# A decoder layer on one core: operands of seven-product units given back one by one, a pair-wise attention state, and other blocks for the left operands' sums

## The chip, the cores and the metric

The kernel runs on 1 core of one Trainium2 chip. The metric is the device time of one execution in microseconds (us), as the median of several runs. Five engines work at once: TensorE (PE in the profile; PEld is its weight load), VectorE (DVE), ScalarE (ACT), GpSimd (POOL) and SyncE (SP), which issues the transfers. Each engine takes its own instructions strictly in its listed order.

## What is computed

One layer of a decoder, 1024 positions of 1024 channels in float32. All matrices are float32 in HBM.

```python
h = rmsnorm(x, pre_mix_g);  z = h @ w_in          # 7696 columns
# z: GLA q,k (256 each), v, out-gate (512 each), forget (16); short conv B,C,x (512 each);
#    dilated q,k,v (1536 each)
y_gla = gla_branch(...)       # linear attention: state = state*decay + k^T v, o = q state + intra part
y_sc  = sc_b * causal_dwconv(sc_c * sc_x)
y_dil = dilated_branch(...)   # rotary q,k; three strided windows
gates = sigmoid(h @ w_gate + b_gate)              # 3 x 1024 columns
x = x + rmsnorm(sum(gates * (branch @ w_branch)) @ w_mix_out)
h = rmsnorm(x, pre_ffn_g)
y = (gelu(causal_dwconv(h @ w_ff_gate) + b) * (h @ w_ff_up)) @ w_ff_down   # 2816 wide
x = x + rmsnorm(y, post_ffn_g)
```

## The kernel before, in words

A float32 product is made of three matmuls: each operand is split into a rounded part (`wh`, a ScalarE copy, L158) and the rest (`wl`, a VectorE subtraction, L159), and high x high, high x low and low x high are added up in PSUM.

**Units of seven products.** Large projections go in units of 256 columns (`seven`, L266 to L323). A unit cuts its 1024 x 256 weights and the activations into 2 x 2 blocks and makes the result from seven block products in place of eight. The activations' block sums (`T`, `FT`) are made once per stage; the weights' sums s1 (L279), s2 (L281), s1' (L283) and A11 - A21 (L285) are made by GpSimd for each unit. The seven operands (A11, A12, s1, s2, s1', A11 - A21, A22, numbered 0 to 6) are each split by L158 and L159. A product is 12 matmuls of 512 columns (L295). On TensorE a unit's products run in the order

    X0 of this unit, X6 of the unit before, Y1, Z2, X3, Z4, X5

where X, Y and Z are PSUM banks and the digit is the operand. X accumulates on: X6 adds to what X5 left, so it can't start until VectorE has read X after X5 (the addition into c22, L315). Between X5 and X6 TensorE has only X0 of the next unit. Z4 is read by the addition into c12 (L313), Y1 by the one into c11 (L304). Each finished quarter goes to a `use` function.

**Places of the operands.** Before, operands 0 to 3 of a unit lie in one pair of tiles (`wh`, `wl`) and 4 to 6 in another, two tiles of each kind in all:

```python
for i in range(2):
    sets.append([wp.tile([128, 4, 4, 128], F32R, name=n, tag=n) for n in ("wh", "wl")])
op = lambda i: (sets[i // 4][0][:, i % 4], sets[i // 4][1][:, i % 4])
```

A tile is written again only when every reader of it is done: operands 0 to 3 of the next unit wait for X3, and 4 to 6 of a unit for X6 of the unit before, which runs behind X0. The raw weights (`raw`, three buffers of 512 KB, loaded by SyncE) come free when the last split of their unit is done.

**Where units run.** Thirty in the input stage (about 75 to 660 us): short conv and gates (the `use` of the short conv's x is L455 and on), then the block that makes cosine and sine on VectorE and ScalarE (L466 to L484), then 12 "turned" units (dilated q and k) mixed with 7 light gate units, then two for the GLA q and k. A turned unit's `use` (`rope_out`, L494) makes, for each quarter, two ScalarE copies of half the partitions (L498, L499), a product with cosine on VectorE (L505), a product with sine on GpSimd (L506) and a VectorE addition (L507). Twenty units run in the feed-forward network (FFN, about 1370 to 1765 us): for c = 1 to 10 one of the gate, whose `use` makes the convolution (L1278 to L1283), and one of the up projection, whose `use` multiplies and calls `forms`.

**`forms` (L1289)** makes left operands for the down projection: a store of quarter a11, of a22 and of a12 as each is made, and at the last quarter four GpSimd results (L1295), each stored: number 5 into a22 (which the store `keep(c, 4, a22)` still reads), 7 into a21, 6 into a11, 3 into a12.

**GLA scan (L797 to L826).** For each of 8 blocks of 128 positions and each of 4 heads: an intra product (L805, 128 rows of weights, 128 columns) and, from block 1, a product with the state (L807, 64 rows, 128 columns), alternating; then four products of 64 weight columns for the new state (L812), and two VectorE operations for it (L817). A float32 matmul call is two passes in the profile. After the scan: `rstd` on VectorE, then per piece a VectorE scaling (L836), a GpSimd product (L838) and four transposes on TensorE (L842).

**What sets the order.** The program states the work in the order of the code; a scheduler at build time then sets the order on each engine, by priorities and by when places come free. So a change of places moves instructions on all engines.

Of the kernel before, what the change touches and what calls it, by code (L numbers as in the profile page):

```python
# [72 lines left out]
def trunk(ctx: ExitStack, tc, x, positions, w_in, w_alpha_up, b_alpha, gla_norm_g, sc_conv_w,  # L73
# [12 lines left out]
    def pt(tag, name):  # L86
        return psum.tile([128, 512], F32, name=name, tag=tag,
                         bufs={"g": 4, "s": 2, "t": 1, "o": 1}[tag])

    def slot(tag, shape, dt=F32, name=None):  # L90
        return main.tile(shape, dt, name=name or tag, tag=tag)
# [174 lines left out]
    def seven(src, c0, B, Ts, tmp, dst, use):  # L266
# [5 lines left out]
        s1, s2 = [t.rearrange("p (k c) -> p k c", k=4) for t in tmp]  # L272
        sets = []
        for i in range(2):
            sets.append([wp.tile([128, 4, 4, 128], F32R, name=n, tag=n) for n in ("wh", "wl")])
        op = lambda i: (sets[i // 4][0][:, i % 4], sets[i // 4][1][:, i % 4])
        split(*op(0), A11)
# [41 lines left out]
        def rest():  # L319
            prod(X, op(6), tt(3), False)  # L320
            use(1, 0, X)
        pending.append(rest)


# [107 lines left out]
    block_sums(H, fr, TS)  # L432
    gemm_by_part(first_units, H, "gt", 256, lambda c, h, ps: gate_out(0)(c, h, ps, ring()))


# [354 lines left out]
    for bp in range(4):  # L790
# [5 lines left out]
        ins = S.activation(kin[:, 2 * bp:2 * bp + 2], p.rearrange("p (b c) -> p b c", c=256), AF.Copy)  # L796
    ssg = sm.tile([128, 32], F32, name="ssg", bufs=1)  # L797
    state = None
    states = slot("t2", [128, 2, 2, 128], name="states")
    for b in range(8):  # L800
        po = [pt(tag, "go")[:, :256].rearrange("p (a e) -> p a e", a=2) for tag in "ot"]
        for h in range(4):
            bs = slice((h % 2) * 64, (h % 2) * 64 + 64)
            p = po[h % 2][:, h // 2]
            PE.matmul(p, Sb[:, b, h], gv[:, b, h * 128:h * 128 + 128], start=True, stop=b == 0)  # L805
            if b:
                PE.matmul(p, qk[bs, h // 2, b * 128:b * 128 + 128], state[bs, h // 2], start=False, stop=True)  # L807
        if b < 7:
            p2 = pt("s", "gst")[:, :256].rearrange("p (a e) -> p a e", a=2)
            for h in range(4):  # L810
                bs = slice((h % 2) * 64, (h % 2) * 64 + 64)
                PE.matmul(p2[bs, h // 2], kin[:, b, h * 64:h * 64 + 64], gv[:, b, h * 128:h * 128 + 128],  # L812
                          start=True, stop=True)
            new = states[:, b % 2]
            for a in range(2):
                if b:
                    V.scalar_tensor_tensor(new[:, a], state[:, a], dec[:, a, b:b + 1], p2[:, a],  # L817
                                           op0=OP.mult, op1=OP.add)
                else:
                    V.tensor_copy(new[:, a], p2[:, a])  # L820
            state = new
        for h in range(4):
            S.activation(gv[:, b, h * 128:h * 128 + 128], po[h % 2][:, h // 2], AF.Square,
                         accum_out=ssg[:, 4 * b + h:4 * b + h + 1])
        for w in range(2):
            V.tensor_copy(gv[:, b].rearrange("p (a w e) -> p a w e", w=2, e=128)[:, :, w], po[w])  # L826
    rg = rstd(ssg, 128, 32)
# [461 lines left out]
    def forms(c, y, il):  # L1289
# [12 lines left out]
        if il == (1, 0):  # L1302
            keep(c, 2, a12)
            made(5, a22, a21, a22, OP.add)
            made(7, a21, a11, a21)
            made(6, a11, a22, a11)
            made(3, a12, a12, a11)

# [16 lines left out]
    for il in ((0, 0), (1, 1), (1, 0)):  # L1325
        forms(0, ys, il)

    ring = halves_ring(("t2", "t0", "t1"))
    yring = Ring([fb[:, i] for i in (0, 1, 3)])
# [194 lines left out]
```

## Time and profile before

| what | value |
|---|---|
| median of 3 runs (their range) | 1985.59 us (1982.05 to 1987.25) |
| the profiled execution | 1988.03 us, span 1986.2 us |
| TensorE busy / weight loads | 1900.2 us (96%) / 1602.9 us (81%) |
| VectorE / ScalarE / GpSimd busy | 66% / 44% / 38% |
| mean granted clock of TensorE | 0.986 |

Busy time counts an instruction from its start to its modelled end; a busy TensorE can still be at a lower clock. "Idle before, releaser" is the time in which the engine did nothing ahead of an instruction, and the instruction that let it go on. Idle time of an engine other than TensorE costs something only where TensorE waits behind it.

### The profile page before, as it was taken

The page shows a single profiled execution, that of the slowest core. Times are in us where ns is not written, and L with a number is a line of the kernel's source. Part 1 is how long each engine was busy: PE and PEld are TensorE (multiplying, and loading weights), DVE is VectorE, ACT ScalarE, POOL GpSimd, SP SyncE. Part 2 cuts the span into 40 slices and gives each one's busy share as a digit, 9 for nine tenths or more (in the row PEclk, how much of TensorE's full clock was granted, in tenths as well). Part 3 has the DMA queues.
Part 4 walks back from the last instruction along what each step waited for, and adds up shares of the span by engine and source line. Part 5 has one row for each costly group of instructions (what it writes and reads, how often), then busy time and mean ns, then how long its engine had stood idle before and what let it go on. Part 6 is the DMA issues. An engine that isn't in the chain of part 4 may idle for free.

```text
span 1986.2 us, 26265 instructions
## 1 busy us (share of the span) xinstructions
PE 1900.2 (96%) x9705; PEld 1602.9 (81%) x9705; DVE 1312.6 (66%) x1913; ACT 875.6 (44%) x1618; POOL 759.6 (38%) x457
## 2 busy tenths in 40 slices
PE   6999999999999999999999998998999999999997
PEld 5988778888777999899688776886878788878885
DVE  8755665677778333578545487677667766779595
ACT  5343345454445323435356633344434443454543
POOL 4522334554545321112214562025444344517172
PEclk9999999999999999999999998999999999999998
DMA  5121323232323424113467554231323233378852
GB/s 174 64 91 59 122 85 122 96 122 94 119 96 120 141 75 150 54 38 102 142 199 233 145 178 148 85 106 49 106 96 117 80 106 107 105 275 317 270 177 101
DMA packets 187072, 251.53 MB, mean 127 GB/s; under 512 B 30017, under 2 KB 121023, under 8 KB 186944
## 3 DMA queue, kind: packets, MB, share of 16 engines
q1 hardware_dynamic: 186944, 249.86, 38.1%
q8 instruction: 76, 1.25, 0.3%
q14 instruction: 52, 0.43, 0.1%
HBM read 183.34 MB, written 66.47 MB: 126 GB/s over the span
## 4 chain that ended last, share of the span: by engine, by line
PE 65%; DVE 18%; issue 5%; DMA 4%; ACT 4%; POOL 4%; SPq 0%; DVEq 0%; ACTq 0%; POOLq 0%
PE sX L295 18%; PE sZ L295 8%; DVE wl L159 6%; PE fX L1467 6%; PE fY L1467 4%; PE sY L295 4%; PE vX L567 3%; PE vZ L567 2%; PE mx L1229 1%; PE mx L1230 1%; PE mx L1228 1%; PE p L198 1%; PE gs L749 1%; PE p L200 1%; PE p L202 1%
## 5 line engine op out<-in xcount | busy, mean ns | idle before, releaser
L159 DVE TENSOR_TENSOR wl<-raw,wh 128x512 fp32r<-128x512 f32 (+1 forms) x214 | 223.8, 1079 | 119.9 <-ACT wh L158 115.3
L295 PE MATMUL sX<-T,wh 128*128 128x512 f32 x720 | 224.1, 393 | 10.7 <-DVE ring L315 10.0
L158 ACT ACTIVATE wh<-raw 128x512 fp32r<-128x512 f32 (+1 forms) x226 | 146.1, 670 | 80.0 <-PE sX L295 57.3
L295 PEld LDWEIGHTS sX<-T,wh 128*128 128x128 f32 x720 | 134.6, 188 | 42.9 <-DVE ring L315 14.2
L295 PE MATMUL sX<-FT,wh 128*128 128x512 f32 x480 | 149.3, 392 | 12.6 <-DVE ring L315 11.2
L295 PE MATMUL sX<-T,wl 128*128 128x512 f32 x360 | 140.7, 391 | 0.0
L506 POOL TENSOR_TENSOR fr<-fr 128x512 f32<-128x512 f32 x48 | 72.0, 1500 | 144.4 <-ACT fr L499 143.0
L295 PEld LDWEIGHTS sX<-FT,wh 128*128 128x128 f32 x480 | 89.2, 188 | 35.7 <-DVE ring L315 15.8
L159 DVE TENSOR_TENSOR wl<-fr,wh 128x512 fp32r<-128x512 f32 x90 | 67.7, 774 | 64.4 <-ACT wh L158 63.6
L158 ACT ACTIVATE wh<-fr 128x512 fp32r<-128x512 f32 (+1 forms) x97 | 61.7, 657 | 77.4 <-PE sX L295 48.5
L295 PE MATMUL sX<-FT,wl 128*128 128x512 f32 x240 | 93.5, 389 | 0.0
L1295 POOL TENSOR_TENSOR fb<-fb 128x512 f32<-128x512 f32 x40 | 57.5, 1438 | 91.2 <-DMA d_fa<-fb 89.6
L279 POOL TENSOR_TENSOR fr<-raw 128x512 f32<-128x512 f32 x30 | 41.4, 1380 | 123.9 <-DMA raw<-in_w_gate_dram 45.3
L159 DVE TENSOR_TENSOR ops<-rw,ops 128x512 fp32r<-128x512 f32 x72 | 67.2, 965 | 27.7 <-ACT ops L158 27.5
L285 POOL TENSOR_TENSOR raw<-raw 128x512 f32<-128x512 f32 x50 | 81.9, 1639 | 0.0
L295 PEld LDWEIGHTS sX<-T,wl 128*128 128x128 f32 x360 | 67.9, 189 | 14.5
L507 DVE TENSOR_TENSOR ring<-ring,fr 128x512 f32<-128x512 f32 x48 | 56.2, 1171 | 30.8 <-POOL fr L506 29.3
L295 PE MATMUL sZ<-T,wh 128*128 128x512 f32 x240 | 73.9, 389 | 0.0
L1467 PE MATMUL fX<-ops 128*128 128x512 f32 x312 | 73.8, 391 | 0.0
L302 ACT ACTIVATE ring<-sX 128x512 f32<-128x512 f32 x48 | 28.5, 594 | 95.7 <-PE sX L295 78.9
L1467 PEld LDWEIGHTS fX<-ops 128*128 128x128 f32 x312 | 59.0, 189 | 12.3
L279 POOL TENSOR_TENSOR fb<-raw 128x512 f32<-128x512 f32 x20 | 26.3, 1313 | 106.4 <-DMA raw<-in_w_ff_gate_dram 74.6
(552 smaller groups left out, 5650.9 us busy)
## 6 DMA issues: line engine op xcount, KB each, us to landing
rw<-in_w_ff_down_dram SPq DMA_DIRECT2D x99, 256.0 KB
raw<-in_w_in_dram SPq DMA_DIRECT2D x48, 512.0 KB
rw<-d_fa SPq DMA_DIRECT2D x77, 256.0 KB
d_fa<-fb SPq DMA_DIRECT2D x70, 256.0 KB
raw<-in_w_gate_dram SPq DMA_DIRECT2D x24, 512.0 KB
d_sig<-ring SPq DMA_DIRECT2D x48, 256.0 KB
d_qk<-ring SPq DMA_DIRECT2D x48, 256.0 KB
raw<-in_w_ff_gate_dram SPq DMA_DIRECT2D x22, 512.0 KB
```

Source lines behind the costliest of these rows:

```text
L158: S.activation(h, src, AF.Copy)
L159: eng.tensor_tensor(l, src, h.bitcast(F32), op=OP.subtract)
L198: PE.matmul(ps[h], a, xs[h][0][:, kx, :], start=st, stop=False)
L279: G.tensor_tensor(s1, A21, A22, op=OP.add)
L285: G.tensor_tensor(A21, A11, A21, op=OP.subtract)
L295: PE.matmul(ps, a[x][:, k], b[y][:, k], start=first and k == 0 and n == 0, stop=k == 3 and n == 2, skip_group_check=not first)
L302: S.activation(c11, X, AF.Copy)
L506: G.tensor_tensor(sw, sw, sin[:, hs], op=OP.mult)
L507: V.tensor_tensor(as_(o), as_(o), perm(sw), op=OP.add)
L567: PE.matmul(o, b[y][:, k, ts], a[:, x, k], start=first and t % 2 == 0 and k == 0 and n == 0, stop=k == 3 and n == 2, skip_group_check=not ...
L1295: G.tensor_tensor(o, p, q, op=op)
L1467: PE.matmul(P[t], o[:, a, ts], o[:, b], start=st, stop=c + k == NCH - 1 and x == 2, skip_group_check=i not in (2, 1, 5))
```

## The change

The diff is whole. Line numbers of the new file differ a little: L304, L310, L313, L315 become L302, L308, L311, L313; L279 to L285 become L277 to L283; L498 to L507 become L503 to L512; L1295 becomes L1305; the scan's L805, L807, L812 become L815, L812, L820; L838 becomes L848.

```diff
--- before.py
+++ after.py
@@ -270,10 +270,8 @@
         r0, r1 = wload([v[:, :4, c0:c0 + 256], v[:, 4:, c0:c0 + 256]], [8, 256])
         A11, A21, A12, A22 = r0[:, :, :128], r0[:, :, 128:], r1[:, :, :128], r1[:, :, 128:]
         s1, s2 = [t.rearrange("p (k c) -> p k c", k=4) for t in tmp]
-        sets = []
-        for i in range(2):
-            sets.append([wp.tile([128, 4, 4, 128], F32R, name=n, tag=n) for n in ("wh", "wl")])
-        op = lambda i: (sets[i // 4][0][:, i % 4], sets[i // 4][1][:, i % 4])
+        ops = [sops() for i in range(7)]
+        op = lambda i: ops[i]
         split(*op(0), A11)
         split(*op(1), A12)
         G.tensor_tensor(s1, A21, A22, op=OP.add)
@@ -320,6 +318,11 @@
             prod(X, op(6), tt(3), False)
             use(1, 0, X)
         pending.append(rest)
+
+    def op_places():
+
+        ts = [[wp.tile([128, 4, 4, 128], F32R, name=n, tag=n) for n in ("wh", "wl")] for i in range(2)]
+        return Ring([(h[:, i], l[:, i]) for h, l in ts for i in range(4)])
     pending = []
@@ -432,6 +435,8 @@
     block_sums(H, fr, TS)
     gemm_by_part(first_units, H, "gt", 256, lambda c, h, ps: gate_out(0)(c, h, ps, ring()))
+    sops = op_places()
+
     for jp in range(2):
         cx = [fr[:, 0], fr[:, 1]]
@@ -795,35 +800,40 @@
                              PQ[:, 2 + a, (2 * bp + bb) * 128:(2 * bp + bb) * 128 + 128], ident)
         ins = S.activation(kin[:, 2 * bp:2 * bp + 2], p.rearrange("p (b c) -> p b c", c=256), AF.Copy)
     ssg = sm.tile([128, 32], F32, name="ssg", bufs=1)
+
+
     state = None
-    states = slot("t2", [128, 2, 2, 128], name="states")
+    states = slot("t2", [128, 2, 2, 256], name="states")
+    G.memset(states, 0.0)
     for b in range(8):
-        po = [pt(tag, "go")[:, :256].rearrange("p (a e) -> p a e", a=2) for tag in "ot"]
-        for h in range(4):
-            bs = slice((h % 2) * 64, (h % 2) * 64 + 64)
-            p = po[h % 2][:, h // 2]
-            PE.matmul(p, Sb[:, b, h], gv[:, b, h * 128:h * 128 + 128], start=True, stop=b == 0)
+        po = [pt(tag, "go")[:, :256] for tag in "ot"]
+        for a in range(2):
             if b:
-                PE.matmul(p, qk[bs, h // 2, b * 128:b * 128 + 128], state[bs, h // 2], start=False, stop=True)
+                PE.matmul(po[a], qk[:, a, b * 128:b * 128 + 128], state[:, a], start=True, stop=True)
+            for w in range(2):
+                h = 2 * a + w
+                PE.matmul(po[a][:, w * 128:w * 128 + 128], Sb[:, b, h], gv[:, b, h * 128:h * 128 + 128],
+                          start=not b and w == 0, stop=True, skip_group_check=b > 0 or w == 1)
         if b < 7:
-            p2 = pt("s", "gst")[:, :256].rearrange("p (a e) -> p a e", a=2)
-            for h in range(4):
-                bs = slice((h % 2) * 64, (h % 2) * 64 + 64)
-                PE.matmul(p2[bs, h // 2], kin[:, b, h * 64:h * 64 + 64], gv[:, b, h * 128:h * 128 + 128],
-                          start=True, stop=True)
+            p2 = pt("s", "gst").rearrange("p (a e) -> p a e", a=2)
+            for a in range(2):
+                PE.matmul(p2[:, a], kin[:, b, a * 128:a * 128 + 128], gv[:, b, a * 256:a * 256 + 256],
+                          start=a == 0, stop=True, skip_group_check=a == 1)
             new = states[:, b % 2]
             for a in range(2):
-                if b:
-                    V.scalar_tensor_tensor(new[:, a], state[:, a], dec[:, a, b:b + 1], p2[:, a],
-                                           op0=OP.mult, op1=OP.add)
-                else:
-                    V.tensor_copy(new[:, a], p2[:, a])
+                for w in range(2):
+                    bs, es = slice(w * 64, w * 64 + 64), slice(w * 128, w * 128 + 128)
+                    if b:
+                        V.scalar_tensor_tensor(new[bs, a, es], state[bs, a, es], dec[bs, a, b:b + 1], p2[bs, a, es],
+                                               op0=OP.mult, op1=OP.add)
+                    else:
+                        V.tensor_copy(new[bs, a, es], p2[bs, a, es])
             state = new
         for h in range(4):
-            S.activation(gv[:, b, h * 128:h * 128 + 128], po[h % 2][:, h // 2], AF.Square,
+            S.activation(gv[:, b, h * 128:h * 128 + 128], po[h // 2][:, h % 2 * 128:h % 2 * 128 + 128], AF.Square,
                          accum_out=ssg[:, 4 * b + h:4 * b + h + 1])
-        for w in range(2):
-            V.tensor_copy(gv[:, b].rearrange("p (a w e) -> p a w e", w=2, e=128)[:, :, w], po[w])
+        for a in range(2):
+            V.tensor_copy(gv[:, b, a * 256:a * 256 + 256], po[a])
     rg = rstd(ssg, 128, 32)
@@ -1301,10 +1311,10 @@
             keep(c, 4, a22)
         if il == (1, 0):
             keep(c, 2, a12)
-            made(5, a22, a21, a22, OP.add)
-            made(7, a21, a11, a21)
-            made(6, a11, a22, a11)
-            made(3, a12, a12, a11)
+            made(7, a11, a11, a21)
+            made(5, a21, a21, a22, OP.add)
+            made(6, a22, a22, a11)
+            made(3, a12, a12, a22)
     first = [wcols(w_fg2, 0), wcols(w_fu2, 0)]
@@ -1325,6 +1335,7 @@
     for il in ((0, 0), (1, 1), (1, 0)):
         forms(0, ys, il)
+    sops = op_places()
     ring = halves_ring(("t2", "t0", "t1"))
     yring = Ring([fb[:, i] for i in (0, 1, 3)])
     STMP = [fb[:, 2, :512], fb[:, 2, 512:]]
```

**Operands.** `op_places` makes eight places, each a `wh` and `wl` quarter of the same two pairs of tiles, in a ring; each unit takes seven, one for each operand. So operand i of a unit goes to the place of operand i - 1 of the unit before, and operand 0 to that of operand 6 two units before. The same number of splits, sums and matmuls is made.

On VectorE, in the input stage, the rows of one turned unit from the addition of Z4 on (L313) to that of the next Y1 (L304), before:

```order
L313 TENSOR_TENSOR ring<-ring,sZ 128x512
L505 TENSOR_TENSOR ring<-fr,ring 128x512
L315 TENSOR_TENSOR ring<-ring,sX 128x512
L507 TENSOR_TENSOR ring<-ring,fr 128x512
L505 TENSOR_TENSOR ring<-fr,ring 128x512
L507 TENSOR_TENSOR ring<-ring,fr 128x512
L159 TENSOR_TENSOR wl<-fr,wh 128x512
L159 TENSOR_TENSOR wl<-raw,wh 128x512 x2
L505 TENSOR_TENSOR ring<-fr,sX 128x512
L304 TENSOR_TENSOR ring<-ring,sY 128x512
```

and the same with the change (L311 to L302):

```order
L311 TENSOR_TENSOR ring<-ring,sZ 128x512
L159 TENSOR_TENSOR wl<-raw,wh 128x512
L510 TENSOR_TENSOR ring<-fr,ring 128x512
L512 TENSOR_TENSOR ring<-ring,fr 128x512
L313 TENSOR_TENSOR ring<-ring,sX 128x512
L159 TENSOR_TENSOR wl<-raw,wh 128x512
L510 TENSOR_TENSOR ring<-fr,ring 128x512
L512 TENSOR_TENSOR ring<-ring,fr 128x512
L159 TENSOR_TENSOR wl<-raw,wh 128x512 x2
L510 TENSOR_TENSOR ring<-fr,sX 128x512
L512 TENSOR_TENSOR ring<-ring,fr 128x512
L302 TENSOR_TENSOR ring<-ring,sY 128x512
```

The cosine product (L505, now L510) of the quarter c12 stood ahead of the addition of X5 (L315) before, and its last addition (L507, now L512) behind it; now both stand ahead of the addition of X5 (L313), and the unit's splits (L159) stand apart, where three and two stood together.

**Left operands' sums.** The four results 7, 5, 6, 3 go to a11, a21, a22, a12 in place of a22, a21, a11, a12. On GpSimd in the FFN, from one unit's last sum to the next unit's, before:

```order
L283 TENSOR_TENSOR fb<-raw,fb 128x512
L1295 TENSOR_TENSOR fb<-fb 128x512 x4
L279 TENSOR_TENSOR fb<-raw 128x512
L281 TENSOR_TENSOR fb<-fb,raw 128x512
L285 TENSOR_TENSOR raw<-raw 128x4x128
L283 TENSOR_TENSOR fb<-raw,fb 128x512
```

and now:

```order
L281 TENSOR_TENSOR fb<-raw,fb 128x512
L1305 TENSOR_TENSOR fb<-fb 128x512 x2
L277 TENSOR_TENSOR fb<-raw 128x512
L279 TENSOR_TENSOR fb<-fb,raw 128x512
L283 TENSOR_TENSOR raw<-raw 128x4x128
L1305 TENSOR_TENSOR fb<-fb 128x512 x2
L281 TENSOR_TENSOR fb<-raw,fb 128x512
```

Before, all four L1295 stood ahead of the next unit's four sums (L279 to L283); now two stand ahead of them and two between the third and the fourth.

**GLA state.** A pair of heads shares a state of 128 rows and 256 columns whose off-diagonal quarters are zero (one GpSimd memset). Per block: two products with the state of 256 columns and 128 rows (L812) in place of four of 128 columns and 64 rows, and two state products of 256 columns (L820) in place of four of 128; the intra products stay four. VectorE makes four state operations of 64 partitions in place of two of 128. What follows the scan on GpSimd, before (the names sg are the buffers that hold the out-gate):

```order
L159 TENSOR_TENSOR wh<-raw,wh 128x1024
L838 TENSOR_TENSOR sg_6096<-sg_6096,gv 128x512 x2
L838 TENSOR_TENSOR sg_6097<-sg_6097,gv 128x512 x2
L838 TENSOR_TENSOR sg_6096<-sg_6096,gv 128x512 x2
L838 TENSOR_TENSOR sg_6097<-sg_6097,gv 128x512 x2
L159 TENSOR_TENSOR wl<-raw,wl 128x1024
```

and now:

```order
L848 TENSOR_TENSOR sg_5980<-sg_5980,gv 128x512 x2
L848 TENSOR_TENSOR sg_5981<-sg_5981,gv 128x512
L159 TENSOR_TENSOR wh<-raw,wh 128x1024
L848 TENSOR_TENSOR sg_5981<-sg_5981,gv 128x512
L848 TENSOR_TENSOR sg_5980<-sg_5980,gv 128x512 x2
L848 TENSOR_TENSOR sg_5981<-sg_5981,gv 128x512 x2
```

One split of 1024 columns (L159), which stood ahead of all of the products (L838, now L848), now stands between the third and the fourth.

## Rows read from the trace of the kernel before

**Rows 1.** The profile page: busy time of each engine, and the chain that ended last.

```profile
PE 1900.2 (96%) x9705; PEld 1602.9 (81%) x9705; DVE 1312.6 (66%) x1913; ACT 875.6 (44%) x1618; POOL 759.6 (38%) x457
...
PE 65%; DVE 18%; issue 5%; DMA 4%; ACT 4%; POOL 4%; SPq 0%; DVEq 0%; ACTq 0%; POOLq 0%
```

**Rows 2.** Busy time by stretch: start:end length, then each engine's busy us (instructions), granted clock.

```profile
210.00:280.00 70.00, 63.85 (x272) 51.68 (x271) 47.17 (x51) 29.21 (x45) 21.79 (x12) 0.98 0.31 105
280.00:660.00 380.00, 373.39 (x1631) 306.17 (x1630) 266.19 (x290) 186.01 (x319) 191.12 (x125) 1.00 0.33 111
570.00:580.00 10.00, 8.75 (x31) 7.10 (x32) 8.73 (x10) 5.12 (x9) 4.03 (x3) 0.83 0.25 77
1390.00:1765.00 375.00, 365.49 (x1600) 299.35 (x1599) 263.99 (x353) 164.09 (x279) 160.06 (x111) 1.00 0.33 113
```

**Rows 3.** The waits of TensorE: who waits, for whom, us in total, times, longest.

```profile
PE sX L295 <- DVE ring L315: 21.1, 18, 2.3
```

**Rows 4.** The waits of GpSimd, same columns.

```profile
POOL fb L1295 <- DMA d_fa<-fb: 89.6, 19, 24.7
```

**Rows 5.** Timeline, GpSimd and TensorE, 224 to 233 us: start, length, instruction, [idle before <-releaser].

```profile
224.09 1.78 POOL L279 TENSOR_TENSOR fr<-raw 128x512 f32<-128x512 f32 x1 [14.39 <-DMA raw<-in_w_gate_dram]
...
232.14 0.74 PE L295 MATMUL sX<-T,wh 128*128 128x512 f32 x2 [2.29 <-DVE ring L315]
```

**Rows 6.** Busy time between two starts, of tile sX alone: one product.

```profile
449.64:452.37 2.73, 2.73 (x14) 2.25 (x13) 0.68 (x1) 0.00 (x0) 1.00 0.00 0
```

**Rows 7.** Timeline, VectorE, ScalarE, GpSimd, turned units (444 to 458 us, and one row at 287).

```profile
287.85 1.76 DVE L507 TENSOR_TENSOR ring<-ring,fr 128x512 f32<-128x512 f32 x1 [1.19 <-POOL fr L506]
...
444.89 3.34 DVE L159 TENSOR_TENSOR wl<-raw,wh 128x512 fp32r<-128x512 f32 x2 [1.45 <-ACT wh L158]
...
452.76 1.08 DVE L507 TENSOR_TENSOR ring<-ring,fr 128x512 f32<-128x512 f32 x1 [0.62 <-POOL fr L506]
453.75 2.17 DVE L505 TENSOR_TENSOR ring<-fr,ring 128x512 f32<-128x512 f32 x1
...
457.81 1.29 DVE L159 TENSOR_TENSOR wl<-raw,wh 128x512 fp32r<-128x512 f32 x2
...
450.71 0.63 ACT L499 ACTIVATE fr<-ring 64x512 f32<-64x512 f32 x1
...
451.42 1.30 POOL L506 TENSOR_TENSOR fr<-fr 128x512 f32<-128x512 f32 x1 [0.82 <-ACT fr L499]
```

**Rows 8.** Timeline, GpSimd, VectorE and TensorE, FFN, 1454 to 1466 us.

```profile
1454.40 1.62 POOL L1295 TENSOR_TENSOR fb<-fb 128x512 f32<-128x512 f32 x1 [3.01 <-DMA d_fa<-fb]
...
1460.68 1.55 DVE L159 TENSOR_TENSOR wl<-fb,wh 128x512 fp32r<-128x512 f32 x1 [0.15 <-ACT wh L158]
...
1464.42 0.68 DVE L315 TENSOR_TENSOR ring<-ring,sX 128x512 f32<-128x512 f32 x1
...
1465.16 0.73 PE L295 MATMUL sX<-FT,wh 128*128 128x512 f32 x2 [1.88 <-DVE ring L315]
```

**Rows 9.** Busy time, tile go alone, one block of the scan.

```profile
944.90:948.30 3.40, 3.34 (x16) 2.37 (x16) 0.00 (x0) 0.63 (x4) 1.00 1.04 247
```

**Rows 10.** Timeline of TensorE, 932 to 953 us.

```profile
932.55 1.72 PE L749 MATMUL gs<-lv 128*128 128x128 f32 x14
...
952.89 0.66 PE L812 MATMUL gst<-gv,gqk 128*64 128x128 f32 x8
```

**Rows 11.** Busy time, line 921 alone: calls of 256 columns.

```profile
1006.67:1007.53 0.86, 0.86 (x4) 0.56 (x3) 1.00 0.10 38
```

**Rows 12.** Timeline, TensorE and GpSimd, 968 to 984 us.

```profile
975.49 0.48 PE L807 MATMUL go<-states,gqk 64*128 64x128 f32 x2
...
983.28 0.66 PE L842 MATMUL yT<-cst,sg 128*128 128x128 f32 x4 [0.95 <-POOL sg L838]
...
968.92 2.35 POOL L159 TENSOR_TENSOR wh<-raw,wh 128x1024 fp32r<-128x1024 f32 x1 [42.87 <-ACT wh L158]
981.63 4.96 POOL L838 TENSOR_TENSOR sg<-sg,gv 128x512 f32<-128x512 f32 x3 [10.36 <-DMA dA<-d_qk]
```

## The prediction

> **What bounds the kernel now.** I read the page first: TensorE is busy for 96% of the span, and it holds 65% of the chain that ended last, with VectorE next at 18% [rows 1]. So time can be won only where TensorE stands still, runs at the lower clock, or is busy with less than it could do. I then cut the span into the stages that the change touches [rows 2]. In 210 to 280 us TensorE is busy for 63.85 of 70 us at a mean clock of 0.98; in 280 to 660 us for 373.39 of 380; in the FFN (1390 to 1765 us) for 365.49 of 375. That is 6.15, 6.61 and 9.51 us of idle time. The waits say what for: 18 waits of the X product for VectorE's addition L315, 21.1 us in all [rows 3]. That is X6 waiting for the addition of X5 into c22. Its cover is one product, X0: 2.73 us [rows 6].
>
> Why the addition is late is seen in two places. At 232.14 us X6 waits 2.29 us; GpSimd's first weight sum had come at 224.09, after 14.39 us without the raw weights [rows 5]. In the FFN GpSimd waits 3.01 us for a store before the last of the four L1295; the sums of the next unit stand behind it, VectorE's splits behind the sums (1.55 us each there), and the addition of X5 behind the splits, at 1464.42; X6 begins at 1465.16 after 1.88 us idle [rows 8]. Such store waits are 89.6 us on GpSimd in all [rows 4].
>
> **The change, part by part.** The sum is against the profiled execution, 1988.0 us, which is 2.4 above the median of the runs; I subtract from the median.
>
> *Operands one by one.* No instruction is added; the splits are spread, about one behind each product, almost a unit ahead of their use. So at most one split stands between the addition of Z4 and that of X5. The last split of a unit, which gives its raw buffers back, no longer waits for X6 of the unit before, but for X5: X6 and the X0 ahead of it, 2 x 2.73 = 5.46 us earlier, and the loads start earlier by that.
>
> In 210 to 280 us there are 6.15 us of idle time and 0.02 x 70 = 1.4 us of clock, 7.5 together. The stall at the cosine block I expect to stay, at its 2.29 us or a little more, because VectorE's long block stands there still: 2.5. Gain 5.0 (bounds 0 and 7.5).
>
> In 280 to 660 us the old 6.61 us go, and a new wait comes. In the 12 turned units the addition of X5 now stands behind the rope's last addition (L512), which waits for GpSimd (L511), which waits for two ScalarE copies, which wait for the addition of Z4 (the orders of VectorE in the section on the change). Counted from the end of Z4, with the uncontended durations of [rows 7, 8]: hand-over 0.2, addition of Z4 0.68, two copies 2 x 0.63, sine product 1.30, last addition 1.08, addition of X5 0.68: 5.2, with about 0.05 to 0.1 for each of five hand-overs 5.5 to 5.7. It is needed after X5 and X0, 5.46 less 0.2 for the hand-over to TensorE: 5.26. I take 0.4 us of stall for each, 12 x 0.4 = 4.8; the lower end is nothing (what hides it is X0, 2.73 us). Gain 6.6 - 4.8 = 1.8 (bounds 6.6 and, below, the fourth rival's).
>
> Here VectorE and GpSimd hinder each other: two splits beside GpSimd's sums take 3.34 us, two without them 1.29 [rows 7]. The Trainium skill (SBUF — State Buffer, the section SBUF: two separate sides) goes further: of a VectorE operation with two SBUF operands and a GpSimd operation that reads SBUF, the one that starts first holds the shared ports for the whole instruction, and the other is blocked. By that the cosine product would hold back the sine product by about 0.4 us more in each turned unit, by my estimate, and the time would be some 5 us higher. The row at 453.75 (2.17 us for a product that takes 1.07 to 1.47 elsewhere) bears it out in part.
>
> *Left operands' sums.* Four L1295 and four stores as before, but number 7 goes first, into a11, whose store is long done, and two of the four move behind the next unit's third sum. So the 3 us wait at the head is gone, and with it the late splits. The gate unit's convolution steps stand between the additions of Z4 and X5 on VectorE, as before, but need no GpSimd step; I count what they hold up within what stays. Of the 9.51 us of idle time I leave 1.0: gain 8.5 (bounds 4 and 9.5). The stores are as many and as large; two come up to 5 us later and nobody waits for them before the down projection.
>
> *GLA state.* One block's intra and state products take 3.40 us for 16 passes [rows 9], 0.21 us a pass, though the same shape alone takes 1.72 / 14 = 0.12 [rows 10]; alternating between 128 and 64 rows is what differs. With the four L812 (8 passes, 0.66 us [rows 10]) a block is 4.06 us. Now: two state products of 256 columns, 4 passes at 0.86 / 4 = 0.215 [rows 11], 0.86; four intra, 8 x 0.123 = 0.98; two L820, 4 passes, 0.86. Sum 2.70, less by 1.36, and in seven blocks by 9.5. VectorE's two more operations of a block lie beside it; the memset comes once, before.
>
> Part of this is given back. From the last L807 at 975.49 to the first transpose at 983.28 is a chain of 7.8 us through VectorE and GpSimd that doesn't shorten, with 0.95 us idle at its end [rows 12]. The matmuls that fill it are 22 now in place of 27, by the orders of TensorE: 5 x 0.2275 = 1.1 us more idle. And the split that ran at 968.92, long before the first L838, for 2.35 us [rows 12], now stands between the third and fourth of them, which the fourth transposes wait for: 2.4. Net gain 9.5 - 3.5 = 6.0 (bounds 9.5 and, by rival A, 1.0).
>
> The Trainium skill (TensorEngine Tiling (Array Packing), Theoretical Speedup) speaks against this part: products over at most 64 rows can run side by side, up to twice as fast, so merging them into one of 128 with half its rows zero would win nothing. The trace doesn't show that pairing: 0.21 us a pass is slower than the full shape, not faster. Its Key Properties, that a change of tiling mode drains the array, fit the row better, and by it the gain is what I took.
>
> **Sum:** 5.0 + 1.8 + 8.5 + 6.0 = 21.3. 1985.6 - 21.3 = 1964.3, forecast **1964** us (profiled: 1966.7).
>
> **Rivals.**
> *A, the scan keeps its slow passes.* If a pass of 128 columns costs 0.21 us here for its weights' change and not for its rows, the eight intra passes take 1.70, a block 3.42, and the gain is 0.64 x 7 = 4.5, less the 3.5: 1.0. Time 1969. For it: every pass there loads new weights; against it: so does [rows 10]'s row of 14, at 0.12. Chance 0.12.
> *B, the FFN's stall only halves,* because the gate unit's convolution steps, not the sums, hold the addition back (one of them stands right ahead of it in the trace). Gain 4.3 in place of 8.5: 1968.5. Chance 0.10.
> *C, the change doesn't do what it says:* VectorE stays late, since its operations are as many. The stalls of the FFN and of 210 to 280 us stay, the turned units pay 1.0 us each (12 - 6.6 = 5.4 more), the scan gains 6.0: 1985. Chance 0.10.
> *D, slower: the rope holds the addition back in earnest.* If VectorE's own work sets the chain, at its slowest rows (split 1.67, cosine product 2.17, last addition 1.76 [rows 7], and 0.68 twice), it ends at 7.16 us, 1.9 late. Such a stall also costs clock: in 570 to 580 us, after TensorE had idled, the granted clock was 0.83 on the mean, so 1.2 GHz for a third of it and 2.4 for the rest [rows 2], which is 1.7 us. Then 12 x 3.6 = 43 in place of 4.8: 2003. It decides from (21.3 + 4.8) / 12 = 2.2 us a turned unit. Against it: half of the rows are near their uncontended length, and the splits are spread now. Chance 0.06.
>
> **How the numbers follow.** My forecast has 0.62, A 0.12, B 0.10, C 0.10, D 0.06. A measurement of this kernel tells about 0.3% (6 us) from no change. Faster: forecast, A and B, 0.84; same: C, 0.10; slower: D, 0.06. The low end is all idle time gone and nothing given back, 7.5 + 6.6 + 9.5 + 9.5 = 33.1: 1952.5, rounded to 1953. The high end holds A and B together with the unfavourable bound of 210 to 280 us, 1978.5, rounded up to 1980; outside are D and most of C.
>
> **What would show it.** Right: waits of X6 for the addition of X5 fall from 21.1 us to under 8, those in the FFN to about 1; TensorE's idle time in 1390 to 1765 us is under 2; one block's products in the scan take 2.7 us. Wrong: a wait of over 1 us for that addition in each turned unit (D), behind an L512 that GpSimd released; L815 at 0.2 us a pass (A); waits for L313 in the FFN still every c (B). My forecast falls if the time lies above 1975 or under 1955.

## The result, and the profile after

The changed kernel takes 2016.62 us (median of 4 runs, 2010.54 to 2019.63) against 1986.42 us before: the ratio is 1.0144, with a 95% interval of 1.0125 to 1.0162. It is slower by some 30 us, where 21 us of gain were forecast.

The page of the changed kernel, the line of [rows 1]:

```profile
PE 1905.7 (94%) x9649; PEld 1608.9 (80%) x9649; DVE 1322.0 (66%) x1927; ACT 892.0 (44%) x1620; POOL 763.2 (38%) x458
```

TensorE is busy for about as long as before, and its share fell from 96% to 94% of a longer span. Busy time by stretch, TensorE alone (start:end length, busy us (instructions), granted clock, then the share of the transfers and GB/s). The stretches are all units of the input stage, the GLA scan, the transposes behind it, and in the FFN the first units and the rest.

```profile
77.70:707.10 629.40, 590.17 (x2511) 0.98 0.30 98
980.90:1013.00 32.10, 30.77 (x174) 1.00 0.43 123
1013.00:1035.30 22.30, 18.00 (x81) 0.85 0.62 202
1392.50:1443.00 50.50, 39.74 (x152) 0.86 0.23 74
1443.00:1788.00 345.00, 344.19 (x1517) 1.00 0.34 112
```

The same for the first four of them before:

```profile
78.10:667.20 589.10, 575.64 (x2511) 0.99 0.31 104
938.00:983.30 45.30, 44.33 (x247) 1.00 0.40 118
983.30:997.70 14.40, 13.31 (x64) 0.88 0.70 213
1355.90:1401.10 45.20, 38.51 (x151) 0.92 0.24 82
```

The input stage went from 589.1 to 629.4 us. Its idle time is 39.2 us, 13.5 before: that is 25.8 of the 40.3 us lost. The other 14.5 are busy time: as many matmuls as before take 590.17 in place of 575.64 us, at a mean clock of 0.98 in place of 0.99. The scan is shorter (by 13.2 us, table below), the transposes behind it are longer by 7.9. In the FFN, 345 us have 0.8 us of idle time, but the first 50.5 have 10.8 and a clock of 0.86, where the same units had 6.7 us in 45.2 before, at 0.92.

The waits of TensorE, after:

```profile
PE sZ L293 <- ACT ring L305: 36.9, 14, 6.9
...
PE sX L293 <- DVE ring L313: 5.3, 4, 2.6
```

X6's wait for the addition of X5 fell from 21.1 us [rows 3] to 5.3, as forecast. A wait that was 2.8 us before now stands at the head: Z4 waits 36.9 us in 14 places for ScalarE's copy of c22 out of Z (L305), 30.0 of them in 13 places of the input stage. One of them, in a turned unit, by the timelines of GpSimd, VectorE, ScalarE and TensorE (start, length, instruction, [idle before <-releaser]):

```profile
508.88 1.75 POOL L277 TENSOR_TENSOR fr<-raw 128x512 f32<-128x512 f32 x1 [1.71 <-DVE ring L313]
510.60 2.16 POOL L511 TENSOR_TENSOR fr<-fr 128x512 f32<-128x512 f32 x1
512.71 1.29 POOL L279 TENSOR_TENSOR fr<-fr,raw 128x512 f32<-128x512 f32 x1
513.96 2.14 POOL L283 TENSOR_TENSOR raw<-raw 128x512 f32<-128x512 f32 x1
...
508.20 0.68 DVE L313 TENSOR_TENSOR ring<-ring,sX 128x512 f32<-128x512 f32 x1
...
509.40 2.18 DVE L510 TENSOR_TENSOR ring<-fr,ring 128x512 f32<-128x512 f32 x1
512.79 2.15 DVE L512 TENSOR_TENSOR ring<-ring,fr 128x512 f32<-128x512 f32 x1 [1.21 <-POOL fr L511]
514.86 3.49 DVE L159 TENSOR_TENSOR wl<-raw,wh 128x512 fp32r<-128x512 f32 x2
518.27 1.05 DVE L510 TENSOR_TENSOR ring<-fr,sX 128x512 f32<-128x512 f32 x1
519.42 1.06 DVE L512 TENSOR_TENSOR ring<-ring,fr 128x512 f32<-128x512 f32 x1
520.40 0.68 DVE L302 TENSOR_TENSOR ring<-ring,sY 128x512 f32<-128x512 f32 x1
...
514.58 0.63 ACT L158 ACTIVATE wh<-fr 128x512 fp32r<-128x512 f32 x1 [0.54 <-PE sY L293]
521.17 0.63 ACT L503 ACTIVATE fr<-ring 64x512 f32<-64x512 f32 x1 [5.96 <-DVE ring L302]
521.82 0.63 ACT L504 ACTIVATE fr<-ring 64x512 f32<-64x512 f32 x1
522.47 0.63 ACT L158 ACTIVATE wh<-fr 128x512 fp32r<-128x512 f32 x1
523.00 0.58 ACT L305 ACTIVATE ring<-sZ 128x512 f32<-128x512 f32 x1
...
523.64 0.50 PE L293 MATMUL sZ<-H1h,wh 128*128 128x512 f32 x1 [3.49 <-ACT ring L305]
```

Read it from the bottom. Z4 stood still for 3.49 us for L305. Z2 had ended by 517.3 (X3 began then), but L305 came at 523.00, because in ScalarE's order there stand ahead of it the rope's two reads of the quarter c11 (L503, L504) and a split of the next unit. L503 waited 5.96 us for VectorE's addition of Y1 (L302). That came at 520.40, though Y1 had ended by 514.7, since VectorE had first the rope of the quarter c22 of the unit before (L510, L512) and two splits to do, each at about twice its length, 2.18, 2.15 and 3.49 us, beside GpSimd's sums and rope product, and then the rope of c21, at 1.05 and 1.06 us. The Trainium skill (SBUF — State Buffer, SBUF: two separate sides) lets the later of two such operations wait for the shared ports; these rows fit that. Alone, a pair of splits took 1.29 us [rows 7].

The FFN's loss is the same queue with another cause:

```profile
1412.71 0.63 ACT L158 ACTIVATE wh<-raw 128x512 fp32r<-128x512 f32 x1 [5.73 <-DMA raw<-in_w_ff_up_dram]
...
1416.32 0.58 ACT L305 ACTIVATE ring<-sZ 128x512 f32<-128x512 f32 x1
...
1416.95 0.80 PE L293 MATMUL sZ<-F1h,wh 128*128 128x512 f32 x1 [6.88 <-ACT ring L305]
```

Here the split of the next unit's operand 1 stands ahead of L305 and waited 5.73 us for its raw weights; two more splits, of GpSimd's sums, stand between them. Before, such a split could not come yet: by the rule of the two tiles it had to wait for X3. The first unit of the input stage, where there is no rope, lost time in the same way: Z4 waited 4.3 us for L305 behind splits that had waited for raw weights and sums.

Stage by stage, from the start of the first matmul of one stage to that of the next, in us of each kernel's profiled execution. "Input" is the 30 units, "transposes" runs from the first L842 (L852) to the first product of the dilated attention. Other products (L198 to L202) fill in between those of the scan and the transposes: 53 of them lie in the scan and 32 behind it before, 36 and 49 with the change. So the two columns are best read together:

| kernel | input | scan | transposes | FFN units | median of runs |
|---|---|---|---|---|---|
| before | 589.1 | 45.3 | 14.4 | 404.4 | 1986.4 |
| changed | 629.4 | 32.1 | 22.3 | 401.2 | 2016.6 |
| e1 sets in the input stage | 589.7 | 32.1 | 22.5 | 400.1 | 1977.3 |
| e2 reads of c11 after c12 | 630.7 | 32.1 | 22.3 | 400.6 | 2015.3 |
| e3 addition of Y1 before the rope | 613.9 | 32.1 | 21.3 | 401.4 | 2000.7 |
| e4 GLA state alone | 590.1 | 32.1 | 20.6 | 401.5 | 1977.7 |
| e5 raw weights by quarters | 606.2 | 32.1 | 21.3 | 413.6 | 2007.4 |
| e6 left operands' sums alone | 590.3 | 45.3 | 15.1 | 392.4 | 1977.9 |
| e7 GLA state and sums | 586.7 | 32.1 | 21.3 | 392.7 | 1969.0 |
| e8 e1, quarters in the FFN | 590.8 | 32.1 | 20.6 | 414.0 | 1988.9 |
| e9 quarters, X5 before the rope | 591.9 | 32.1 | 20.6 | 418.7 | 1998.3 |
| e10 all orders | 585.8 | 32.1 | 20.6 | 394.3 | 1968.1 |
| e11 all orders, quarters in the input | 582.5 | 32.1 | 22.3 | 394.3 | 1965.7 |
| e12 ScalarE's orders only | 592.8 | 32.1 | 20.6 | 399.6 | 1978.4 |
| e13 VectorE's order only | 632.5 | 32.1 | 22.3 | 417.8 | 2038.6 |

### The profile page after: what moved, and what is told of

It is laid out like the page before. It is cut to its first block, busy times and chain, and to the rows that moved or that the text cites. A ratio compares the mean times of both kernels' runs of the same rounds, so it can differ in the third digit from the quotient of the medians.

```text
span 2017.6 us, 26461 instructions
## 1 busy us (share of the span) xinstructions
PE 1905.7 (94%) x9649; PEld 1608.9 (80%) x9649; DVE 1322.0 (66%) x1927; ACT 892.0 (44%) x1620; POOL 763.2 (38%) x458
## 3 DMA queue, kind: packets, MB, share of 16 engines
q8 instruction: 76, 1.25, 0.3%
## 5 line engine op out<-in xcount | busy, mean ns | idle before, releaser
L159 DVE TENSOR_TENSOR wl<-raw,wh 128x512 fp32r<-128x512 f32 (+1 forms) x214 | 232.6, 1097 | 73.8 <-ACT wh L158 73.5
L158 ACT ACTIVATE wh<-raw 128x512 fp32r<-128x512 f32 (+1 forms) x226 | 152.3, 679 | 245.3 <-PE sX L293 131.2
L277 POOL TENSOR_TENSOR fr<-raw 128x512 f32<-128x512 f32 x30 | 42.9, 1430 | 180.2 <-DMA raw<-in_w_gate_dram 61.9
L511 POOL TENSOR_TENSOR fr<-fr 128x512 f32<-128x512 f32 x48 | 78.7, 1640 | 63.9 <-ACT fr L504 63.9
L158 ACT ACTIVATE wh<-fr 128x512 fp32r<-128x512 f32 (+1 forms) x97 | 63.9, 660 | 86.7 <-PE sY L293 21.5
L1305 POOL TENSOR_TENSOR fb<-fb 128x512 f32<-128x512 f32 x40 | 52.9, 1323 | 123.4 <-DVE fb L1353 88.5
L159 DVE TENSOR_TENSOR wl<-fr,wh 128x512 fp32r<-128x512 f32 x90 | 71.4, 805 | 36.3 <-ACT wh L158 35.6
L512 DVE TENSOR_TENSOR ring<-ring,fr 128x512 f32<-128x512 f32 x48 | 57.5, 1197 | 50.9 <-POOL fr L511 49.3
L159 DVE TENSOR_TENSOR wl<-fb,wh 128x512 fp32r<-128x512 f32 x60 | 58.0, 967 | 45.7 <-ACT wh L158 45.1
L159 DVE TENSOR_TENSOR ops<-rw,ops 128x512 fp32r<-128x512 f32 x72 | 63.2, 903 | 35.5 <-ACT ops L158 35.0
L283 POOL TENSOR_TENSOR raw<-raw 128x512 f32<-128x512 f32 x50 | 86.4, 1729 | 0.0
L293 PE MATMUL sZ<-H1h,wh 128*128 128x512 f32 x120 | 53.0, 442 | 34.6 <-ACT ring L305 30.0
L281 POOL TENSOR_TENSOR fr<-raw,fr 128x512 f32<-128x512 f32 x30 | 48.1, 1603 | 94.9 <-DVE wl L159 92.4
L158 ACT ACTIVATE wh<-fb 128x512 fp32r<-128x512 f32 x60 | 37.9, 632 | 87.1 <-PE sY L293 31.3
```

Source lines behind the costliest of these rows:

```text
L158: S.activation(h, src, AF.Copy)
L159: eng.tensor_tensor(l, src, h.bitcast(F32), op=OP.subtract)
L277: G.tensor_tensor(s1, A21, A22, op=OP.add)
L281: G.tensor_tensor(s1, A12, s2, op=OP.subtract)
L283: G.tensor_tensor(A21, A11, A21, op=OP.subtract)
L293: PE.matmul(ps, a[x][:, k], b[y][:, k], start=first and k == 0 and n == 0, stop=k == 3 and n == 2, skip_group_check=not first)
```

## The experiments

T1 put the loss on ScalarE's queue, T2 on the places themselves (VectorE late whatever the order), T3 on late raw weights.

**The three parts, each without the others.** In e1 the input stage's units keep the two sets:

```diff
-        ops = [sops() for i in range(7)]
-        op = lambda i: ops[i]
+        if sops is None:
+            sets = [...]
...
-    sops = op_places()
+    sops = None
```

> The changed kernel, but the 30 units of the input stage keep the operands in two sets as before; the 20 units of the FFN use the eight places. Theory T1 (the loss is made in the input stage, where on ScalarE the copy of c22 that Z4 waits for stands behind the rope's and the gates' reading of c11, which waits for VectorE's addition of Y1): the 27 us of waits of Z4 for that copy and the clock lost with them go, the input stage falls back by about 40 us, the scan's and the FFN's gains stay, about 1976 us. Rival T2 (eight places cost time wherever they are used, the FFN's too): over 1990 us, and the FFN no shorter than before. Rival T3 (the raw weights come late whatever the places): Z4's waits stay.

1977.31 us, ratio 0.9944 (0.9927 to 0.9960). The input stage is back at 589.7 us: the loss against the kernel before is made by the places in the input stage. The other two parts alone, e4 (the scan's lines of the diff) and e6 (the four `made` lines), and both together without the places, e7:

> The kernel before with the pair-wise GLA state alone. The scan is shorter by about 13 us as in the changed kernel, and 8 us are given back in the transposes behind it, if that comes from the shorter scan itself: 1979 to 1982 us. If the given-back time came from the moved split on GpSimd or from the order that the other parts brought: 1972 to 1975 us. If a pass of 128 columns stayed at 0.21 us: 1985 us or more.

> The kernel before with only the four left operands' sums put in the other blocks. If the store that the first of them waits for is what makes the FFN's stall, the 9.5 us of idle time in the FFN fall to under 4: 1979 to 1983 us. If the order on GpSimd (all four ahead of the next unit's sums) is what matters and stays without the new places: 1985 to 1989 us.

> The kernel before with the pair-wise GLA state and the left operands' sums in the other blocks, without the new places. If the parts add up: the GLA state's 10 us and what the sums' blocks give alone, 1971 to 1976 us. Below the version with eight places in the FFN only (1977.3), if the places give nothing there; above it, if they are what takes the FFN's stall away.

e4: 1977.74 us, 0.9951 (0.9933 to 0.9969). e6: 1977.92 us, 0.9949 (0.9932 to 0.9967); the FFN's units take 392.4 us in place of 404.4, and TensorE stands still there for 7.3 us:

```profile
1365.20:1757.70 392.50, 385.21 (x1685) 1.00 0.32 109
```

e7: 1969.04 us, 0.9902 (0.9875 to 0.9929). Each of the three times is 1 to 2 us below the range in which its part should have come out. e4 gains 10.3 us, of which its scan and transposes make 7.0; the rest was not followed up. So the parts nearly add up, and the sums' blocks need no new places to take the FFN's stall away. With the places as well (e1) the FFN takes 400.1 us: there they cost 7 us.

**Two orders that were not enough.** e2 puts the reads of c11 behind the copy of c12 on ScalarE, e3 the rope of the unit before behind the addition of Y1 on VectorE:

```diff
-        S.activation(c12, X, AF.Copy)
-        use(0, 0, c11)
+        i12 = S.activation(c12, X, AF.Copy)
+        with tc.issue_after(i12.ins):
+            use(0, 0, c11)
```

```diff
-        V.tensor_tensor(c11, c11, Y, op=OP.add)
+        i11 = V.tensor_tensor(c11, c11, Y, op=OP.add)
+        with tc.issue_after(i11.ins):
+            last_use()
...
-            use(1, 0, X)
+            held_uses.append(lambda: use(1, 0, X))
```

> The changed kernel, with one order added on ScalarE: what reads the quarter c11 stands behind the copy of c12, as the code has it. T1: the waits of Z4 for the copy of c22 in 280 to 707 us fall from 27 us to under 5, the time by 27 us and some of the 8 us of clock, to 1980 to 1990 us. T2 (VectorE is late in itself, because its splits and GpSimd's sums hinder each other): the wait goes to X5, X6 or Y1, in sum nearly as long, and the time stays within 8 us of 2016.6. T3 (late raw weights): no change.

> The changed kernel, with one order added on VectorE: the rope of the quarter c21 of the unit before stands behind the addition of Y1 in place of ahead of it. T1 names that addition as what ScalarE's queue waits for, so it comes some 2 to 4 us earlier, and the waits of Z4 fall from 27 us to under 12: 1990 to 2003 us. T2 (VectorE is late because the splits ahead of that addition take 3.5 us beside GpSimd's work, not because of the rope): less than 5 us of it go. T3: no change.

e2: 2015.33 us, 1.0141 (1.0118 to 1.0164). The waits of Z4 for the ring's copy fell, but X5 now waits 29.6 us in 16 places for the copy of c12 (L308). ScalarE and TensorE in e2:

```profile
520.97 0.58 ACT L305 ACTIVATE ring<-sZ 128x512 f32<-128x512 f32 x1
528.27 0.63 ACT L158 ACTIVATE wh<-fr 128x512 fp32r<-128x512 f32 x1 [6.72 <-POOL fr L281]
528.80 0.58 ACT L308 ACTIVATE ring<-sX 128x512 f32<-128x512 f32 x1
...
529.43 1.22 PE L293 MATMUL sX<-T,wh 128*128 128x512 f32 x2 [3.44 <-ACT ring L308]
```

The copy of c12 came late behind a split (L158 at 528.27) that had waited 6.72 us for GpSimd's sum s1'. I took this for T2 at first. e3: 2000.69 us, 1.0067 (1.0041 to 1.0094); the input stage is 15.5 us shorter, near the upper end for T1. (In e3 one quarter of the short convolution's product is overwritten before it is used, since its reading moved behind a copy into the same buffer. So e3 computes something else there, with the same amount of work, and its time is a weaker witness than the others.)

**Earlier raw weights.** A raw buffer comes free with the split of its unit's last operand, so late splits make late loads and late sums. GpSimd waited 58.5 us for them in the changed kernel's units of 280 to 707 us (36.8 and 21.7), 3.3 before. e5 loads four quarters into six places:

```diff
-        r0, r1 = wload([v[:, :4, c0:c0 + 256], v[:, 4:, c0:c0 + 256]], [8, 256])
-        A11, A21, A12, A22 = ...
+        A11, A12, A21, A22 = [quarter() for i in range(4)]
+        for o, k, c in ((A11, 0, 0), (A12, 4, 0), (A21, 0, 128), (A22, 4, 128)):
+            nc.sync.dma_start(o, v[:, k:k + 4, c0 + c:c0 + c + 128])
```

> The changed kernel, but a unit's raw weights are loaded as four quarters of 256 KB into six places of their own, so that a quarter is given back when its own last reader is done. Theory T4, from the two runs with one order more: the stall only moves with the orders because VectorE itself is late between the additions of X5 and Y1; it is late because a unit's second raw load goes out only after the split of operand 6, so GpSimd's sums fall into the window of the rope and both engines take up to twice as long. With quarters the loads go out 5 us or more earlier, the sums too, and the waits of Z4 and X5 for ScalarE's copies in 280 to 707 us fall from 27 us to under 10: 1978 to 1995 us. If it is the order of the splits alone (one behind each product) that makes VectorE late (T2): no more than 8 us of change. Smaller loads that cost more than they give: over 2016 us.

2007.44 us, 1.0091 (1.0061 to 1.0120): above the range of T4. The input stage falls by 23 us to 606.2, Z4's waits there to 1.7 us, but a new wait stands in each of the 12 turned units, and the FFN is 12 us longer. Waits of TensorE in e5's input stage, and two of the twelve:

```profile
PE sX L294 <- DVE ring L314: 22.6, 13, 3.4
```

```profile
563.09 0.72 PE L294 MATMUL sX<-T,wh 128*128 128x512 f32 x2 [1.71 <-DVE ring L314]
...
585.41 0.74 PE L294 MATMUL sX<-T,wh 128*128 128x512 f32 x2 [2.97 <-DVE ring L314]
```

That is rival D's wait in rival D's place (X6, for the addition of X5 behind the rope), 22.0 us in twelve places from 298 to 649 us, which in the changed kernel, with its stalls of Z4, had come to only 0.7 us after 280 us. e8 put the quarters into the FFN of e1, e9 put the rope of c12 behind the addition of X5:

> The version with two sets in the input stage and eight places in the FFN, and in the FFN the raw weights loaded as quarters. The loss at the FFN's start (Z4 5.7 us behind ScalarE, which waits for a load that stands behind five stores) and the waits for the addition of X5 are both late loads by T4: they fall to under 3 us in sum, 1965 to 1972 us. If not: 1975 to 1980 us.

> The changed kernel with the input stage's raw weights loaded as quarters, and one order more: on VectorE the rope of the quarter c12 stands behind the addition of X5, in place of ahead of it. With quarters alone the input stage took 606 us (629 in the changed kernel, 589 before), and X6 then waited for that addition in each of the 12 turned units, 0.6 to 3.4 us. Theory: these waits are the rope's (addition of Z4, two copies on ScalarE, sine product on GpSimd, last addition), and with it behind they fall from 22 us to under 8, the input stage to 585 to 595 us, the kernel to about 1980 to 1990 us. If VectorE's own work is what is late: the waits stay over 15 us or come back as waits of Z4 or X5, 600 us or more in the input stage.

e8: 1988.93 us, 1.0005 (0.9990 to 1.0020), a miss: the FFN's units take 414.0 us, with X6's waits back. Quarters as loads don't pay there; why was not followed up. e9: 1998.31 us, 1.0060 (1.0039 to 1.0080), above the 1980 to 1990 that I expected: the input stage takes 591.9 us as expected, but the FFN, which I had not thought of, is worse at 418.7, with Z4 and X5 waiting for ScalarE (9.8 and 12.3 us there).

**All that stands ahead of ScalarE's copies.** e10 puts the next unit's splits, and the reads of c11, behind the copies of c22 and c12 on ScalarE, and the rope of c12 behind the addition of X5 on VectorE. Loads and places are those of the change:

```diff
-        split(*op(0), A11)
+        behind(0, op(0), A11)
...
-        split(*op(4), s1)
+        behind(1, op(4), s1)
...
+        copies[:] = [i22.ins, i12.ins]
+        with tc.issue_after(i12.ins):
+            use(0, 0, c11)
...
+        with tc.issue_after(ix.ins):
+            use(0, 1, c12)
...
+    def behind(i, o, src):
+        with tc.issue_after(copies[i]) if copies else nullcontext():
+            split(*o, src)
```

Here `i22`, `i12` are the two copies, `ix` the addition of X5. e11 has the input stage's quarters as well; e12 has ScalarE's orders alone, e13 VectorE's alone.

> The changed kernel with orders only: on ScalarE the copies of c22 and c12 stand ahead of the next unit's splits (operands 0 to 3 behind the copy of c22, 4 to 6 behind that of c12) and of what reads c11; on VectorE the rope of c12 stands behind the addition of X5. Loads as in the changed kernel. If the stalls are only a matter of what stands ahead of the copies: the waits of Z4 and X6 go, 12 us at the FFN's start as well, and the time is 1965 to 1980 us. If the late raw loads are what counts: the splits come later still, X0 waits for them (operand 0), and the input stage stays over 605 us, over 1990 us in all.

> The same orders, with the input stage's raw weights loaded as quarters. If both causes count, late loads and what stands ahead of the copies and of the addition of X5, this is the one in which the eight places cost nothing: input stage 580 to 590 us, 1960 to 1975 us in all. If the places cost something of themselves in the turned units: input stage over 595 us.

> The changed kernel with ScalarE's orders only (the copies of c22 and c12 ahead of the next unit's splits and of what reads c11); nothing ordered on VectorE. If ScalarE's queue is the cause: the input stage 583 to 592 us and the kernel 1965 to 1976 us, as with both orders (585.8 and 1968). If the rope ahead of the addition of X5 on VectorE is as much of it: waits of X6 of over 10 us more, 1980 to 1995 us.

> The changed kernel with VectorE's order only (the rope of c12 behind the addition of X5). If ScalarE's queue is the cause: the waits of Z4 and X5 for ScalarE's copies stay over 20 us, over 2000 us. If the rope's place on VectorE is: 1975 to 1990 us.

e10: 1968.07 us, 0.9898 (0.9876 to 0.9920), 48.5 us less than the changed kernel with the same instructions. Its waits and its two stages of units:

```profile
PE sX L293 <- DVE ring L315: 10.7, 9, 2.3
```

```profile
79.80:665.60 585.80, 573.45 (x2510) 1.00 0.33 105
1348.00:1742.40 394.40, 386.11 (x1684) 0.99 0.34 111
```

e11: 1965.68 us, 0.9890 (0.9872 to 0.9908), no different from e10 by the intervals, so the late weights are not a cause of their own: with e10's orders GpSimd still waits 22.6 us for them in 280 to 700 us. e12: 1978.43 us, 0.9960 (0.9945 to 0.9975), between the two ranges of its expectation. The input stage takes 592.8 us, just above the first range, and what is left there is X6's wait:

```profile
PE sX L293 <- DVE ring L315: 11.2, 6, 2.5
```

e13: 2038.57 us, 1.0253 (1.0235 to 1.0271), and ScalarE's copies are waited for as in the changed kernel or longer:

```profile
PE sZ L293 <- ACT ring L305: 40.0, 23, 6.4
...
PE sX L293 <- ACT ring L308: 12.4, 9, 1.6
```

The orders given on ScalarE do it: alone they give 38 of the 48 us. VectorE's order is worth 10 more behind them, and costs 22 without them, 16.6 of these in the FFN. One turned unit of e12 shows why:

```profile
559.33 0.60 ACT L305 ACTIVATE ring<-sZ 128x512 f32<-128x512 f32 x1 [2.94 <-PE sZ L293]
...
561.65 0.68 DVE L302 TENSOR_TENSOR ring<-ring,sY 128x512 f32<-128x512 f32 x1
...
563.39 1.28 DVE L159 TENSOR_TENSOR wl<-raw,wh 128x512 fp32r<-128x512 f32 x2
```

VectorE's addition of Y1 (L302) is still late, 5.1 us behind the end of Y1, against 5.7 in the changed kernel's unit above. But the copy of c22 (L305) now waits for nothing but Z2, comes 2.3 us ahead of that addition, and Z4 does not wait. So VectorE's lateness alone (T2) does not make the stall. One thing goes with it: a split's VectorE half follows its ScalarE half, so these orders also put VectorE's splits back together, behind the addition of Y1 (L159 at 563.39). T1 stands, in a wider form than I had stated it (the reads of c11 alone are not enough; no run orders the splits alone). Three versions are the fastest of all, e7, e10 and e11, by 1.0 to 1.1% against the kernel before, and can't be told apart by their intervals; e7 has none of the new places.

## Why the prediction was wrong

*Operands one by one, 280 to 660 us: the step that failed.* I counted as the only new wait the addition of X5 behind the rope's chain, 4.8 us in all, and named X0 as its cover. I read the new order of VectorE alone. The splits that come "almost a unit ahead" are also ScalarE copies, and they and the rope's early reads stand in ScalarE's order ahead of the copies of c22 and c12, each waiting for a late engine: VectorE (5.96 us), GpSimd (6.72 in e2) or a load (5.73). e12 shows it: with ScalarE's order put right the input stage takes 592.8 us. For the whole stage I forecast 6.8 us gained; 40.3 were lost. From the unit that begins at 275.6 us before (281.4 now), 1.8 gained were forecast and 34.1 lost. In the units up to 210 us, for which I had no term at all, 8.1 were lost, 6.7 of them in the first unit. Between these I had 5.0 gained and it is 1.9: the wait at the cosine block came as forecast (2.58 us for 2.5), but the clock stayed at 0.97. These two stretches, before and after in turn:

```profile
209.70:275.60 65.90, 59.75 (x254) 0.97 0.31 104
217.40:281.40 64.00, 61.26 (x260) 0.97 0.33 107
275.60:667.20 391.60, 384.99 (x1682) 1.00 0.33 112
281.40:707.10 425.70, 395.06 (x1675) 0.98 0.32 104
```

*Rival D* had the sign (2003 us) and, with 43 us for the turned units, about the size, but for another wait; that is luck. Its own wait was there behind the other: 22.0 us in 12 units when the weights came earlier (e5), 1.8 us a unit, where its contended chain gave 1.9. In the changed kernel itself it is not what cost the time.

*Raw weights.* The step that loads start 5.46 us earlier did not hold. The sums' waits for weights in 280 us and on rose from 3.3 to 58.5 us. I put that down to the last split, which comes late with VectorE; no run shows it by itself.

*Left operands' sums.* Right in the mechanism: alone they take 12.0 us off the FFN, and in the change 345 us of it have 0.8 us of idle time, for the 1.0 that I left. Not counted were the first units, where the places' early split blocked ScalarE (6.88 us) and the clock fell to 0.86: they take 5.3 us more than before, the rest 8.5 less as forecast, so 3.2 us in place of 8.5.

*GLA state.* Right. The intra and state products of a block take 1.75 us where they took 3.40 [rows 9]; I had 1.84:

```profile
988.52:990.27 1.75, 1.75 (x12) 1.62 (x12) 0.38 (x1) 0.63 (x4) 1.00 1.06 310
```

The intra passes are at about 0.11 us now that every product has 128 rows, so rival A is out. Whether the alternation was slow or the 64 rows themselves, no run separates. The Trainium skill (TensorEngine Tiling (Array Packing), Theoretical Speedup) would have had the products over 64 rows gain from running side by side; merging them with half the rows zero was faster here. The scan and the transposes behind it together hold 8.9 us less of busy time (I had 9.5) and 3.6 more of idle time (I had 3.5); net 5.3 for 6.0. (The scan alone is 13.2 shorter and the transposes 7.9 longer, because 17 other products moved behind it.) The split of 1024 columns among L848 is where I put it, and the fourth transposes wait behind it:

```profile
1016.31 2.81 POOL L159 TENSOR_TENSOR wh<-raw,wh 128x1024 fp32r<-128x1024 f32 x1
...
1020.84 1.12 PE L852 MATMUL yT<-cst,sg 128*128 128x128 f32 x4 [2.38 <-POOL sg L848]
```

In e4, without the other parts, the transposes take 20.6 us, so most of it belongs to the GLA part. How much is the shorter scan and how much the split stays open, since in e4 the split stands among these products too (2.82 us at 975.91).

*Rivals B and C* did not come: X6's waits fell as forecast, from 21.1 to 5.3 us.

## What to carry to other kernels

Giving buffers back sooner lets a scheduler bring the next step's work forward, and not only on the engine that one had in mind. On an engine that takes its instructions in order, such work may then stand ahead of the copy that the busiest engine waits for next, and wait for something late itself; so read the new order of each engine that empties PSUM, not only of the one whose wait is to go. Where buffers are given back sooner, put those copies first by an explicit order, and look whether the buffers are needed at all: here the other two parts gave as much without them.

## What was not expected of the hardware

Operations of VectorE and GpSimd side by side took about twice as long where their work came to lie together: the rope's product and its last addition 2.18 and 2.15 us, where most others of the trace take 0.67 to 1.25. These rows are not new with the change: 7 of the 48 products and 6 of the 48 additions took over 2.1 us before, 7 and 7 after. So the prediction's 1.07 to 1.47 us for the product "elsewhere" is too narrow. And the cost of a stall goes on behind it: in the FFN's first 50.5 us TensorE was idle for 10.8 us, 6.88 of them in one wait, and the granted clock was 0.86, a mean of its two levels of 1.2 and 2.4 GHz; in the 345 us behind, with 0.8 us idle, it was 1.00.
